# A hybrid attention layer: the third unit's queries and gate values as seven half-size products, the slot cut in two

## The chip, the cores and the metric

The kernel runs on one core of a Trainium2 chip. A core has a matrix engine (TensorE, PE in the profile, with PEld for its weight loads), a vector engine (VectorE, DVE), a scalar engine (ScalarE, ACT), GpSimd (POOL) and SyncE (SP), which here does nothing but issue DMAs. The metric is the device time of one execution in microseconds (us); lower is better.

## The reference, cut to what matters

One decoder layer over 2048 tokens of width 1024. The input is normalised and modulated to `h`, and one projection of `h` gives all that the two attention groups need:

```python
proj = jnp.einsum('bsd,de->bse', h, w_in[l])
gq, gk, gv, ga, gz, sq, sk, sv, sz = split_cols(proj, COL_SIZES)
o_gla = gla_chunked(gq, gk, gv, log_a)            # gated linear attention, 4 heads
o_gla = rmsnorm(o_gla, g_gla_head) * silu(gz)
o_swa = sliding_window_sink_attention(rope(sq), rope(sk), sv, sinks)   # 8 query heads
o_swa = o_swa * silu(sz)
y = jnp.einsum('bse,ed->bsd', jnp.concatenate([o_gla, o_swa], axis=-1), w_out[l])
x = x + gate * y                                   # then a last rmsnorm
```

The queries `sq` and the gated group's values `gv` (the "gate values" of the change) are 512 columns each, so side by side they are one product of 2048 x 1024 tokens by 1024 x 1024 weights.

## The kernel before, in words

**Numbers in two parts.** All is float32 in and out. A large product splits each factor into a rounded high part and the rest (`hh`, `hl` for the tokens; two parts of each weight), both of type float32r, and adds three products (`mm3`: high-high, high-rest, rest-high). One product of 128 x 128 by 128 x 512 is one MATMUL instruction.

**Units and slots.** The 2048 tokens go in four units `u` = 0 to 3 of 512. A unit's projection is cut into slots: `kv` (keys, values and the low-rank gate), `sz0`, `sz1`, `gz0`, `gz1` (the gates), `qk0`, `qk1` (the gated group's queries and keys), `sq` and `gv`. A 512-column slot done plainly takes 4 token tiles x 8 pieces of k x 3 = 96 MATMULs, so `sq` and `gv` take 192 in a unit. `ORDER` (L58) lists the slots of units 1 and 2, `ORDER_F` those of a unit in `FAST` (L59, L60). When the slots that a piece of attention needs are there, the main loop (from L1720) records it: sliding-window tiles (`swa_tile`, PE tiles `pq`, `psc`, `ppt`, `ppo`), the linear attention (`gla`, tiles `gaT`, `pz`, `pk`, `pc`, `pu`, `po`, `pms`).

**Seven products for eight.** Unit 3 alone is in `FAST`. There `sq` and `gv` are one slot `sqgv`: the 512 x 1024 tokens and the 1024 x 1024 weights are seen as 2 x 2 blocks, and Strassen's algorithm (in Winograd's form, `SEVEN`, L65) makes seven block products of 24 MATMULs each, 168 in all. It needs sums of token blocks, `s1` to `s4`, sums of weight blocks, `t1` to `t4`, and sums of the results.

- The token sums (`prepare`, L715) are made on DVE from the slot `sz0` on, in four steps i. A step adds `hh` and `hl` back into two buffers (tag `xs`, two buffers, tile `S`), forms the sums, splits one buffer into parts (`Shh`, `Shl`) and stores the other in DRAM (`sd`), from where `second` loads it later for `s1` and `s4`. The next step's buffers are free when that store has landed. The parts live in the five pairs of `h` buffers that the next unit's tokens, or the output weights, take afterwards.
- The weight sums (`late_cols(k)`, L672, k from 0 to 3, called 4 to 7 in `LATE_AT`) are made once: per k four loads of `wct`, four subtractions on POOL, four splits (ACT `wtxt`, DVE `wtyt`) and eight stores to `wt` in DRAM.
- The results are added as they leave PSUM (`done`, L785), by DVE, 14 adds of 128 x 512; the plain slots are taken out by DVE's rotary products (`sq`) and by ACT copies (`gv`).

**Weights.** Unit 0 splits the weights and stores both parts in DRAM (`wc`). Later units load each tile again, 1 MB as two DMAs of 512 KB, into five buffers (`WB`, L61; `ahead`, L909): the load of a tile waits until PE is done with the tile five before. A plain 512-column slot loads 4 MB; `sqgv` loads 14 tiles, 14 MB. The output weights are made alike by `late_gate` and `late_rows(k)` (k 0 to 3: four loads of `wor`, 14 stores to `woc`) and loaded by `last_rows` near the end; then come the output products (`ya`, `ys`, `yl`).

**What sets the order.** Nothing runs as it is written. Each operation is recorded (class `Order`), with the engine, a planned length, what it reads and writes, and a priority: its place in the program plus a "lift" (negative is earlier). `issue` (L229) then lays all operations out by a list schedule and writes a fixed order for each engine. SP works through one queue in that order: a DMA whose data or buffer isn't ready holds all behind it. All instructions carry the lines of the helper (L454 for MATMUL, L397 for the rest), so the tiles' names tell what is what: `w_b` are weight blocks loaded from `wc`, `w_t` the sums loaded from `wt`, `pf` the PSUM tiles of the seven products, `pn` and `pt` those of plain slots.

Of the kernel before, what the change touches and what calls it, by code (L numbers as in the profile page):

```python
# [53 lines left out]
NORM_AT0 = 'sq'  # L54
NORM_AT = 'sq'
ORDER0 = ['sz1/0', 'gz1/0', 'kv', 'sz1/1', 'gv', 'sq', 'qk1', 'gz1/1']
ORDER = ['sz0', 'kv', 'sz1', 'sq', 'qk0', 'gv', 'gz0', 'qk1', 'gz1']
FAST = (3,)  # L58
ORDER_F = {2: ['sz0','kv','sz1','sqgv','qk0','gz0','qk1','gz1'], 3: ['sz0','kv','sqgv','sz1','qk0','gz0','qk1','gz1']}  # L59
STATS_AT = 0  # L60
AGAIN_LIFT = 800  # L61
PREP_LIFT = 400
PREP_AT = 'sz0'
SEVEN = (("a11", "b11"), ("a12", "b21"), ("s2", "t2"), ("s3", "t3"), ("a22", "t4"), ("s1", "t1"), ("s4", "b22"))
LATE_AT = {(1,'sz0'):'gate',(1,'sz1'):0,(1,'sq'):4,(1,'gv'):5,(1,'qk1'):6,(2,'sz0'):7,(2,'sz1'):1,(2,'gv'):2,(2,'gz0'):3}  # L65
WO = ("b11", "b21", "t1", "b22", "t2", "t3", "t4")
# [3 lines left out]
LIFT = 600  # L70
# [332 lines left out]
def layer_kernel(ctx, tc, small, x, xT, w_ada, w_gate, b_gate, w_in, w_dec, w_out, g_fin, out):  # L403
# [289 lines left out]

    def slot_f(u):
# [17 lines left out]
        stream.extend([lambda n=n, j=j: load(n, j) for n in range(7) for j in range(2)])  # L712
        return lambda i, n, k: tiles[n, k // 2][:, k % 2, i]
# [461 lines left out]
    gv = {}  # L1175
# [538 lines left out]
    for i, (u, slot) in enumerate(todo):  # L1714
# [112 lines left out]
```

## Time and profile before

| what | value |
|---|---|
| median of 3 runs | 822.41 us (822.40 to 823.12) |
| profiled execution, its own time | 822.16 us |
| its span, first to last instruction | 820.4 us |
| granted TensorE clock | 0.998 |
| moved by DMA | 221.79 MB, 270 GB/s mean |
| unit 2 (its first `sz0` product to unit 3's) | 328.9 to 492.9 us |
| unit 3 (to its last `gz1` product) | 492.9 to 647.6 us |
| output products after that | 647.6 us to the end |

Busy time of an engine is the union of its instructions' times; MATMULs overlap one another (about 0.39 us each, a new one every 0.23 us), so PE's busy time is not a sum of lengths. "Idle before" gives the time in which the engine had nothing running ahead of an instruction, and what released it. SPq rows are DMAs as SP issues them; a long one was held at the head of the queue.

### The profile page before, as it was taken

Reading aid. Unit: us, or ns where it says so; the run is one execution under the profiler, and the core shown is the slowest. Engines: PE = TensorE matmul, PEld = TensorE weight load, DVE = VectorE, ACT = ScalarE, POOL = GpSimd, SP = SyncE. Lnnn points to the kernel's source line nnn. Section 1 sums busy time; section 2 is a strip of 40 time slices with the busy share of each in tenths; the row PEclk is TensorE's granted clock in tenths of the full one; section 3 lists DMA queues with packets and bytes.
Section 4 is the critical chain, followed back from the end, with each engine's and each line's share of the span. In section 5 each row is a group of like instructions: output and inputs, shape, how many; then the busy total and the mean of one; then the engine's idle time right before and its main releaser. Section 6 shows DMA issues by size and latency. Waiting matters only on the chain.

```text
span 820.4 us, 13492 instructions
## 1 busy us (share of the span) xinstructions
PE 803.6 (98%) x4262; PEld 669.0 (82%) x4262; DVE 626.8 (76%) x1234; ACT 528.0 (64%) x1315; POOL 377.7 (46%) x458
## 2 busy tenths in 40 slices
PE   8899999999999999999999999999999999999996
PEld 7788788888888878878887888788888888888885
DVE  6998467777668988675788958877686577989985
ACT  4769856899546787857488766453786636444432
POOL 3813225476435766656569542343644332223300
PEclk9999999999999999999999999999999999999999
DMA  9979998738286597998977967899999945664422
GB/s 357 372 257 379 380 388 290 265 130 325 100 291 233 195 371 251 303 336 307 348 278 269 324 225 235 286 353 402 340 350 346 309 128 178 218 201 153 165 99 78
DMA packets 101917, 221.79 MB, mean 270 GB/s; under 512 B 10531, under 2 KB 28502, under 8 KB 99158
## 3 DMA queue, kind: packets, MB, share of 16 engines
q1 hardware_dynamic: 101558, 220.67, 75.8%
q8 instruction: 34, 0.56, 0.3%
q14 instruction: 37, 0.30, 0.1%
q10 hardware_dynamic: 288, 0.26, 0.1%
HBM read 156.80 MB, written 64.09 MB: 269 GB/s over the span
## 4 chain that ended last, share of the span: by engine, by line
PE 76%; DMA 7%; DVE 4%; ACT 4%; issue 2%; POOL 1%; SPq 1%; DVEq 0%; POOLq 0%; ACTq 0%
PE pt L454 23%; PE pn L454 15%; PE ya L454 10%; PE ys L454 9%; PE pf L454 5%; PE ppo L454 3%; PE psc L454 3%; PE po L454 2%; PE ppt L459 2%; DMA xt<-in_xT 1%; DMA xn<-in_x 1%; PE pc L454 1%; PE pms L454 1%; DMA wr_gv<-in_w_in 1%; PE pu L454 1%
## 5 line engine op out<-in xcount | busy, mean ns | idle before, releaser
L454 PE MATMUL pt<-hh,w_gz 128*128 128x512 f32 x224 | 75.7, 397 | 0.0
L454 PE MATMUL pt<-hh,w_qk 128*128 128x512 f32 x224 | 74.5, 398 | 0.0
L454 PE MATMUL pt<-hh,w_sz 128*128 128x512 f32 x224 | 73.6, 397 | 0.3 <-ACT kvr L397 0.3
L397 ACT ACTIVATE ge<-ge 128x512 f32<-128x512 f32 x96 | 60.5, 630 | 9.8 <-DVE ge L397 8.9
L397 ACT ACTIVATE s<-s,nm 128x129 f32<-128x129 f32 x128 | 51.1, 400 | 18.4 <-DVE nm L397 17.8
L454 PE MATMUL pn<-w_gv,hh 128*128 128x512 f32 x192 | 62.0, 397 | 0.2 <-ACT kvr L397 0.2
L454 PE MATMUL pn<-w_sq,hh 128*128 128x512 f32 x192 | 61.7, 395 | 0.0
L397 POOL TENSOR_TENSOR xt<-xt,rstd 128x512 f32<-128x512 f32 x27 | 40.6, 1505 | 28.7 <-DMA xt<-in_xT 24.9
L454 PE MATMUL ys<-woht,m 128*128 128x512 f32 x168 | 53.6, 392 | 0.0
L397 POOL TENSOR_TENSOR o<-o,zs 128x128 f32<-128x128 f32 x64 | 33.5, 542 | 39.8 <-DVE o L397 29.8
L454 PE MATMUL pn<-w_kv,hh 128*128 128x272 f32 x256 | 50.1, 290 | 0.2 <-ACT zs L397 0.2
L454 PEld LDWEIGHTS pt<-hh,w_sz 128*128 128x128 f32 x224 | 41.7, 188 | 9.2 <-ACT kvr L397 0.5
L454 PE MATMUL ya<-wohb,m 128*128 128x512 f32 x152 | 49.0, 390 | 0.0
L454 PEld LDWEIGHTS pt<-hh,w_gz 128*128 128x128 f32 x224 | 41.7, 188 | 8.5 <-issue 0.2
L454 PEld LDWEIGHTS pt<-hh,w_qk 128*128 128x128 f32 x224 | 41.7, 188 | 8.3
L397 POOL TENSOR_TENSOR s<-s,den 128x512 f32<-128x512 f32 x32 | 37.7, 1181 | 16.1 <-DVE den L397 15.3
L454 PE MATMUL pt<-hl,w_gz 128*128 128x512 f32 x112 | 44.5, 397 | 0.0
L454 PE MATMUL pt<-hl,w_sz 128*128 128x512 f32 x112 | 44.4, 396 | 0.0
L454 PE MATMUL pt<-hl,w_qk 128*128 128x512 f32 x112 | 44.3, 396 | 0.0
L397 POOL TENSOR_TENSOR qr<-qr,rope 128x256 f32<-128x256 f32 x32 | 26.4, 846 | 35.4 <-DVE rope L397 25.7
L454 PEld LDWEIGHTS pn<-w_sq,hh 128*128 128x128 f32 x192 | 35.8, 188 | 8.1 <-issue 0.3
L454 PEld LDWEIGHTS psc<-kst,qs 128*128 128x128 f32 x256 | 37.7, 188 | 5.5 <-DVE s L397 1.0
(324 smaller groups left out, 2475.1 us busy)
## 6 DMA issues: line engine op xcount, KB each, us to landing
w_sz<-wc SPq DMA_DIRECT2D x24, 512.0 KB, 6.2
w_qk<-wc SPq DMA_DIRECT2D x24, 512.0 KB, 5.1
w_gz<-wc SPq DMA_DIRECT2D x24, 512.0 KB, 5.1
w_sq<-wc SPq DMA_DIRECT2D x16, 512.0 KB, 7.0
w_gv<-wc SPq DMA_DIRECT2D x16, 512.0 KB, 9.1
w_t<-wt SPq DMA_DIRECT2D x16, 512.0 KB, 7.4
mr<-mixd SPq DMA_DIRECT2D x32, 256.0 KB, 3.6
y<-in_x SPq DMA_DIRECT2D x32, 256.0 KB, 3.3
```

Source lines behind the costliest of these rows:

```text
L397: return order.add(eng, lambda: real(*args, **kw), dur, ins, outs, lock=lock, nbytes=nbytes)
L454: return od.add("PE", lambda: T.matmul(o, l, r, start=start, stop=stop), dur, [l, r] + ([] if start else [o]), [bank if start and bank is ...
L459: return od.add("PE", lambda: T.transpose(o, i, ident), 0.109, [i, ident], [o], mode="few" if o.shape[0] <= 32 else None)
```

## The change

Four things change together.

1. Unit 2 joins `FAST`: its `sq` and `gv` become seven products too. `prepare(2)` is called at its `sz0`.
2. The slot of the seven products is cut: `sqgv` makes the first five (a11 b11, a12 b21, s2 t2, s3 t3, a22 t4: all queries are there after them), a new slot `gvb` makes the last two (s1 t1, s4 b22). Unit 2 has `qk0` between them, unit 3 `qk0` and `qk1`. In both units `sz1` now stands ahead of `sqgv`; before, unit 3 had it behind. What waited for `gv`, and the next unit's `norm`, comes after `gvb`.
3. `LATE_AT` is rewritten: the weight sums (4 to 7) are recorded in unit 1 (second of the four, slots `sz0` and `kv`) ahead of the gate (`qk0`), the output weights (0 to 3) in unit 2 from `gz0` to unit 3's `sz0`. Before, the gate came first, and sums and output weights alternated from unit 1's `sz1` to unit 2's `gz0`.
4. `AGAIN_LIFT`, the priority of `second`, goes from 800 to 600.

```diff
-FAST = (3,)
-ORDER_F = {..., 3: ['sz0','kv','sqgv','sz1','qk0','gz0','qk1','gz1']}
+FAST = (2,3)
+ORDER_F = {2: ['sz0', 'kv', 'sz1', 'sqgv', 'qk0', 'gvb', 'gz0', 'qk1', 'gz1'],
+           3: ['sz0', 'kv', 'sz1', 'sqgv', 'qk0', 'qk1', 'gvb', 'gz0', 'gz1']}
-AGAIN_LIFT = 800
+AGAIN_LIFT = 600
-LATE_AT = {(1,'sz0'):'gate',(1,'sz1'):0,(1,'sq'):4,(1,'gv'):5,...}
+LATE_AT = {(1, 'sz0'): (4, 5), (1, 'kv'): (6, 7), (1, 'qk0'): 'gate', ...}
...
+    SPLIT = 5
+    def part_of(u, slot):
+        at = SPLIT if "gvb" in ORDER_F[u] else len(SEVEN)
+        return range(at) if slot == "sqgv" else range(at, len(SEVEN))
...
-        for n, (a, _) in enumerate(SEVEN):
+        def product(n, a, w):
...
+        def run(slot, w):
+            for n in part_of(u, slot):
+                product(n, SEVEN[n][0], w)
...
-        if u < NU - 1 and name == ("sqgv" if u in FAST else NORM_AT if u else NORM_AT0):
+        if u < NU - 1 and (last_f if u in FAST else name == (NORM_AT if u else NORM_AT0)):
```

How the order moves, first in SP's queue at the start of unit 3's `kv`. Before, the stores of the token sums (`sd`) stand directly ahead of the first product's second weight tile (`w_b_1`):

```order
L397 DMA w_kv_3_1403<-wc 128x544 x2
L397 DMA woc<-woyb_1296 128x512
L397 DMA w_b_0_1407<-wc 128x1024 x2
L397 DMA sd_104<-S_1395 128x512
L397 DMA sd_104<-S_1397 128x512
L397 DMA w_b_1_1432<-wc 128x1024 x2
L397 DMA w_b_0_1433<-wc 128x1024 x2
L397 DMA w_b_1_1434<-wc 128x1024 x2
L397 DMA sd_104<-S_1399 128x512
```

Now, at the same place:

```order
L397 DMA w_kv_3_1420<-wc 128x544 x2
L397 DMA mixd<-o 128x256
L397 DMA sd_105<-S_1412 128x512
L397 DMA woc<-woyt_1361 128x512
L397 DMA w_sz_0_1424<-wc 128x1024 x2
L397 DMA woc<-woyb_1363 128x512
L397 DMA sd_105<-S_1414 128x512
L397 DMA wor_1366<-in_w_out 128x512
L397 DMA woc<-woxt_1364 128x512
L397 DMA w_sz_1_1467<-wc 128x1024 x2
L397 DMA w_b_0_1468<-wc 128x1024 x2
```

The second store now stands ahead of `sz1`'s second tile, and the products' tiles come after it.

The same place in unit 2, SP's queue from the last `kv` tile on. Before, plain weights, token loads for the next unit's statistics (`xn`) and the weight sums under way (`wct` in, `wt` out):

```order
L397 DMA w_kv_3_980<-wc 128x544 x2
L397 DMA wt<-wtyt_829 128x512
L397 DMA wct_890<-in_w_in 128x512
L397 DMA xn_1198<-in_x 128x512
L397 DMA wt<-wtxt_830 128x512
L397 DMA mixd<-qk_834 128x4x128
L397 DMA w_sz_0_984<-wc 128x1024 x2
```

Now:

```order
L397 DMA w_kv_3_993<-wc 128x544 x2
L397 DMA woc<-woxb_1292 128x512
L397 DMA sd_104<-S_985 128x512
L397 DMA w_sz_0_997<-wc 128x1024 x2
L397 DMA woc<-woyb_1293 128x512
L397 DMA sd_104<-S_987 128x512
L397 DMA w_sz_1_1022<-wc 128x1024 x2
L397 DMA w_b_0_1023<-wc 128x1024 x2
L397 DMA w_b_1_1024<-wc 128x1024
L397 DMA sd_104<-S_989 128x512
L397 DMA w_b_1_1024<-wc 128x1024
L397 DMA w_b_0_1025<-wc 128x1024 x2
```

The weight sums are gone from here (they stand in unit 1 now), the statistics' loads come some twelve rows later, and three stores of token sums stand among the weight tiles.

PE's rows in unit 2, where the first token tile of `gv` began, before (one tile `pn` runs through all eight `h` pieces; a piece of sliding-window work, `ppo`, stands between):

```order
L454 MATMUL pn_1231<-w_gv_1_1070,hh_2_811 128x512 x2
L454 MATMUL pn_1231<-w_gv_1_1070,hl_2_812 128x512
L454 MATMUL pn_1231<-w_gv_1_1070,hh_3_814 128x512
L454 MATMUL ppo<-ph,vs 128x512
L454 MATMUL pn_1231<-w_gv_1_1070,hh_3_814 128x512
L454 MATMUL pn_1231<-w_gv_1_1070,hl_3_815 128x512
```

Now, where the second product ends and the third, with token sums, begins (a piece of linear attention, `pms`, stands between):

```order
L454 MATMUL pf_1064<-w_b_0_1025,hh_3_819 128x512 x2
L454 MATMUL pf_1064<-w_b_0_1025,hl_3_820 128x512
L454 MATMUL pf_1064<-w_b_1_1034,hh_5_962 128x512
L454 MATMUL pms<-osq_948,ones_r 128x512
L454 MATMUL pf_1064<-w_b_1_1034,hh_5_962 128x512
L454 MATMUL pf_1064<-w_b_1_1034,hl_5_963 128x512
L454 MATMUL pf_1064<-w_b_1_1034,hh_7_968 128x512 x2
L454 MATMUL pf_1064<-w_b_1_1034,hl_7_969 128x512
L454 MATMUL pf_1069<-w_t_0_1038,Shh_974 128x512 x2
```

A `pf` tile takes four pieces of k, 12 MATMULs, where a `pn` tile takes eight, 24. Unit 2 has 14 `pf` tiles in place of 8 `pn` tiles, 168 MATMULs in place of 192.

More of the change, by code (lines that the diff above doesn't have):

```diff
@@ L57 @@
 ORDER = ['sz0', 'kv', 'sz1', 'sq', 'qk0', 'gv', 'gz0', 'qk1', 'gz1']
-FAST = (3,)
-ORDER_F = {2: ['sz0','kv','sz1','sqgv','qk0','gz0','qk1','gz1'], 3: ['sz0','kv','sqgv','sz1','qk0','gz0','qk1','gz1']}
+FAST = (2,3)
+ORDER_F = {2: ['sz0', 'kv', 'sz1', 'sqgv', 'qk0', 'gvb', 'gz0', 'qk1', 'gz1'], 3: ['sz0', 'kv', 'sz1', 'sqgv', 'qk0', 'qk1', 'gvb', 'gz0', 'gz1']}
 STATS_AT = 0
-AGAIN_LIFT = 800
+AGAIN_LIFT = 600
 PREP_LIFT = 400
@@ L64 @@
 SEVEN = (("a11", "b11"), ("a12", "b21"), ("s2", "t2"), ("s3", "t3"), ("a22", "t4"), ("s1", "t1"), ("s4", "b22"))
-LATE_AT = {(1,'sz0'):'gate',(1,'sz1'):0,(1,'sq'):4,(1,'gv'):5,(1,'qk1'):6,(2,'sz0'):7,(2,'sz1'):1,(2,'gv'):2,(2,'gz0'):3}
+LATE_AT = {(1, 'sz0'): (4, 5), (1, 'kv'): (6, 7), (1, 'qk0'): 'gate', (2, 'gz0'): 0, (2, 'qk1'): (1, 2), (3, 'sz0'): 3}
 WO = ("b11", "b21", "t1", "b22", "t2", "t3", "t4")
@@ L692, in late_cols, with slot_f @@
         part("t4", b[1, 0], b[1, 0], b[1, 1])
-    def slot_f(u):
+    SPLIT = 5
+    def part_of(u, slot):
+        at = SPLIT if "gvb" in ORDER_F[u] else len(SEVEN)
+        return range(at) if slot == "sqgv" else range(at, len(SEVEN))
+    def slot_f(u, slot):
         tiles = {}
@@ L710, in load @@
                 SY.dma_start(f(t[:, k]), f(src))
-        stream.extend([lambda n=n, j=j: load(n, j) for n in range(7) for j in range(2)])
+        stream.extend([lambda n=n, j=j: load(n, j) for n in part_of(u, slot) for j in range(2)])
         return lambda i, n, k: tiles[n, k // 2][:, k % 2, i]
@@ L751, in prepare, with proj_f @@
         return combos, second
-    def proj_f(u, w, combos, qr_of):
+    def proj_f(u, combos, qr_of):
         def left(op, k, p):
@@ L826, in proj_f @@
                 od.lift = 0
+        def run(slot, w):
+            for n in part_of(u, slot):
+                product(n, SEVEN[n][0], w)
+        return run
     def rope_in_place(q, t):
@@ L1652, in layer_kernel @@
     todo = [(0, n) for n in ORDER0] + [(u, n) for u in range(1, NU) for n in (ORDER_F[u] if u in FAST else ORDER)]
-    ws = [slot_f(u) if n == "sqgv" else slot_w(u, n, LIFT if i > 1 else 0) for i, (u, n) in enumerate(todo)]
-    ready_s = {}
+    ws = [slot_f(u, n) if n in ("sqgv", "gvb") else slot_w(u, n, LIFT if i > 1 else 0) for i, (u, n) in enumerate(todo)]
+    ready_s, run_f = {}, {}
     warm(WARM0, None)
@@ L1724, in layer_kernel @@
             qrs[u] = {}
-            proj_f(u, w, ready_s[u], qrs[u])
+            run_f[u] = proj_f(u, ready_s[u], qrs[u])
+            run_f[u](name, w)
+        elif name == "gvb":
+            run_f[u](name, w)
         elif name == "sq":
@@ L1734, in layer_kernel @@
         seen.add((u, slot))
-        seen |= {(u, n) for n in ("sq", "gv") if name == "sqgv"}
+        if name == "sqgv":
+            seen.add((u, "sq"))
+        last_f = u in FAST and name == ("gvb" if "gvb" in ORDER_F[u] else "sqgv")
+        if last_f:
+            seen.add((u, "gv"))
         if half:
@@ L1746, in layer_kernel @@
                               ("Z", 0, ("qk0", "gz0", "gv")), ("Z", 1, ("qk1", "gz1", "gv"))):
-            if (name in need or name == "sqgv") and all((u, n) in seen for n in need):
+            if (name in need or "sq" in need and name == "sqgv" or "gv" in need and last_f) and all((u, n) in seen for n in need):
                 if what == "S":
```

## Prediction

> **What bounds the kernel now.** I read the page first, its busy times and the chain that ended last.
>
> ```profile
> PE 803.6 (98%) x4262; PEld 669.0 (82%) x4262; DVE 626.8 (76%) x1234; ACT 528.0 (64%) x1315; POOL 377.7 (46%) x458
> PE 76%; DMA 7%; DVE 4%; ACT 4%; issue 2%; POOL 1%; SPq 1%; DVEq 0%; POOLq 0%; ACTq 0%
> ```
>
> PE is busy 98% of the span and holds 76% of the chain. A busy PE need not be a fast one, since the MATMULs overlap, so I looked at the pace next: two pieces of the chain in which one slot's products stand alone, the first plain, the second of the seven products.
>
> ```profile
> 98.00 12.75 PE pn L454 x56
> ...
> 560.73 5.49 PE pf L454 x24
> ```
>
> 12.75/56 = 0.228 us and 5.49/24 = 0.229 us for a MATMUL of 512 columns, in both kinds of slot. Then the waits of PE, the longest four of its list, to see what is left besides work:
>
> ```profile
> PE po L454 <- ACT hh L397: 2.3, 2, 2.1
> PE pw L454 <- POOL ones_r L397: 2.1, 1, 2.1
> PE pf L454 <- DMA w_b<-wc: 1.7, 1, 1.7
> PE pk L459 <- DVE qk L397: 1.2, 1, 1.2
> ```
>
> The first two belong to the start, which the change leaves. Of the rest only the third, in unit 3's seven products, is over 1.2 us. So the time is the number of MATMULs by their pace, and the question is whether PE is still fed. For that I read the busy times by stage: unit 2, unit 3, the densest 10 us of DMA that I found, and two stretches inside unit 3 that matter below.
>
> ```profile
> 330.00:492.90 162.90, 161.17 (x898) 134.17 (x897) 122.00 (x224) 115.84 (x287) 100.09 (x114) 1.00 0.84 298
> 492.90:647.80 154.90, 153.13 (x850) 128.04 (x849) 115.34 (x241) 95.39 (x242) 67.60 (x84) 1.00 0.93 326
> 400.00:410.00 10.00, 10.00 (x60) 8.82 (x59) 6.99 (x16) 7.52 (x24) 5.15 (x6) 1.00 1.03 406
> 505.60:516.00 10.40, 10.35 (x85) 9.98 (x86) 8.45 (x24) 4.82 (x13) 1.28 (x4) 1.00 0.46 132
> 516.00:560.00 44.00, 42.29 (x234) 34.65 (x231) 35.88 (x73) 19.55 (x38) 19.59 (x24) 1.00 0.98 353
> ```
>
> After the length come PE, PEld, DVE, ACT and POOL, the clock, the DMA share and GB/s. DVE runs at 75% in both units (122.00/162.90, 115.34/154.90), and DMA is the next limit: 353 GB/s at a share of 0.98 while unit 3's seven products load their weights.
>
> **Part by part.** *Fewer products.* Unit 2's `sq` and `gv` go from 192 to 168 MATMULs (14 `pf` tiles of 12). 24 x 0.229 = 5.5 us leave the engine that sets the end. The other work of PE is the same in number.
>
> [...]
>
> *Unit 3's wait.* SP's queue and PE at the start of unit 3's products, with the landing of the load that PE waited for:
>
> ```profile
> 504.56 0.41 PE L454 MATMUL pn<-w_kv,hh 128*128 128x272 f32 x2
> ...
> 518.52 0.62 PE L454 MATMUL pf<-w_b,hh 128*128 128x512 f32 x2
> ...
> 522.24 0.73 PE L454 MATMUL pf<-w_b,hh 128*128 128x512 f32 x2 [1.71 <-DMA w_b<-wc]
> ```
>
> ```profile
> 504.75 0.80 SPq L397 DMA_DIRECT2D w_b<-wc  x2
> 505.64 10.43 SPq L397 DMA_DIRECT2D sd<-S  x2
> 516.16 3.34 SPq L397 DMA_DIRECT2D w_b<-wc  x6
> 522.89 0.32 SPq L397 DMA_DIRECT2D sd<-S  x1
> ```
>
> ```profile
> 516.16 6.03 DMA w_b<-wc
> ```
>
> The second store of token sums stood 10.43 us at the head of the queue; the tile behind it was issued at 516.16, landed 6.03 us later at 522.19, and PE had wanted it 1.71 us before 522.24, at 520.5. Now `sz1` stands between `kv` and the products, and behind the second store comes `sz1`'s second tile. PE wants that 24 MATMULs after `kv`, at 518.5 + 5.5 = 524.0: 1.8 us to spare. The product's second tile now stands behind the third store: 522.9 + 0.3 + 6.0 = 529.2, wanted at 518.5 + 11.0 (`sz1`) + 1.4 (six MATMULs) = 530.9: 1.7 us to spare. So the wait of 1.7 us goes. It stays, in another place, if the stores come 1 us later each.
>
> *The same chain, new in unit 2.* `prepare` and its stores stand there as in unit 3, with one half of the second tile ahead of the third store, so the spare time is no smaller. What differs is the bytes. From the first store to the last tile of the fifth product the queue holds 17.3 MB by the sizes in its order: tiles 12.6, stores 1.0, statistics' loads (`xn`) 2.1, the rest 1.6. With K the start of `kv`, that last tile is wanted at K + 14.0 (`kv`, 518.52 - 504.56) + 11.0 (`sz1`, 48 x 0.229) + 23.4 (102 MATMULs) + 6.0 (other PE work in the slot, an estimate from the rows below and from 14 small ones) = K + 54.4.
>
> ```profile
> 477.52 1.02 PE pu L454 x16
> ...
> 528.00 1.09 PE pc L454 x16
> ...
> 536.60 1.99 PE po L454 x24
> ```
>
> If the first 10.4 us go at 132 GB/s, as unit 3's did while the store held the queue (1.4 MB), the remaining 15.9 MB take 39.2 us at 406 GB/s or 45.0 us at 353. The tile lands at K + 1 + 10.4 + 39.2 = K + 50.6, in time, or at K + 56.4, 2.0 us late. I take the middle of no wait and 2.0: +1.0 us. For unit 3 the queue holds 17.0 MB (no `xn`, more output weights): none or 1.2 us, I take +0.6.
>
> *DVE and ACT in unit 2.* The token sums and the adds cost what unit 3's did:
>
> ```profile
> L397 DVE TENSOR_TENSOR S<-hh,hl 128x512 f32<-128x512 f32 x8 | 6.6, 822 | 4.2 <-DMA sd<-S 4.1
> L397 DVE TENSOR_TENSOR S<-S,S 128x256 f32<-128x256 f32 x12 | 6.1, 510 | 0.1
> L397 DVE TENSOR_TENSOR Shl<-S,Shh 128x512 fp32r<-128x512 f32 x8 | 6.1, 772 | 1.3 <-PE pms L454 0.7 <-ACT Shh L397 0.6
> L397 DVE TENSOR_TENSOR S<-S 128x256 f32<-128x256 f32 x4 | 1.7, 415 | 0.0
> L397 DVE TENSOR_TENSOR v<-pf,v 128x512 f32<-128x512 f32 x4 | 2.7, 686 | 2.4 <-PE pf L454 2.4
> L397 DVE TENSOR_TENSOR wtyt<-wct,wtxt 128x512 fp32r<-128x512 f32 x16 | 14.2, 890 | 2.9 <-ACT wtxt L397 1.4 <-issue 1.1 <-DMA w_kv<-wc 0.3
> L397 DVE TENSOR_TENSOR wtyt<-wct,wtxt x16: 678/691/1777, 327.7 to 427.4; 128x512 fp32r<-128x512 f32 x16
> ```
>
> 6.6 + 6.1 + 6.1 + 1.7 = 20.5 us, and 14 adds x 0.686 = 9.6. But the 14.2 us of splitting weight sums, all but the first of which ran in unit 2 (327.7 to 427.4), move to unit 1. Net 122.0 + 30.1 - 14.2 = 138 us of DVE in some 157: 88%. A `pf` tile lives 12 MATMULs, 2.75 us, and its adds take 0.69 or 1.4; PE's list has no wait for them in unit 3. I cost this at nothing; PE's own work covers it, and if the cover goes, it shows as the late stores below.
>
> *Moves.* Unit 2's queue holds 2.2 MB less than before (45.9 for 48.1, weight sums out, the larger tiles in), all from unit 3's first tile on holds 4.3 MB more (70.1 for 65.8, late output weights). Sums made early in unit 1 load POOL, busy 46% of the span. The 1.2 us wait of `pk` stood in unit 2 and may go or come back elsewhere: 0, from -1.2 to +1.2.
>
> Sum: 822.16 (the profiled execution; the runs' median, 822.41, is as good as the same) - 5.5 - 1.7 + 1.0 + 0.6 = **816.6 us**.
>
> **The rivals.**
>
> *DMA becomes the bound; the gain is given back.* The queue is already at 0.93 to 0.98 where this change adds. If it goes at 340 GB/s, between unit 3's mean of 326 and the 353, unit 2's last tile lands at K + 11.4 + 46.8, 3.8 us late, unit 3's (15.6 MB after the slow start) at K + 57.3, 2.9 us late; the 4.3 MB more in the last stage take 12.2 us at 353 where 7% of 154.9, 10.8 us, are free: 1.4 more. 822.16 - 5.5 - 1.7 + 8.1 = 823.1: no difference that counts. For it: the shares. Against: before, 16.8 MB went through the same place with one wait, and that came of the queue's order.
>
> [...]
>
> *The stores of token sums come later, and weights wait behind them; slower.* The steps were 8.6 us on average ((522.89 - 505.64)/2). In unit 2 the second half of the product's second tile lands at K + 1.1 + two steps + 6.0 and is wanted at about K + 27.1, so this decides from 10.0 us a step. At 14 us, were DVE 5 us a step busier with other work: `sz1`'s second tile 1.9 us late, that half tile 6.1 more, the tile behind the fourth store 1.1: 9.1 us. In unit 2 alone that is 822.16 - 5.5 - 1.7 + 9.1 = 824.1, in both units 833.2. For it: DVE at 88%, and thin spare times. Against: the weight sums are out of the way, and unit 3's steps were made beside much the same work.
>
> **How the numbers follow.** A difference of 0.2%, 1.6 us, is about what a measurement here can tell from none: faster is below 820.8, slower above 824.1. My forecast, with waits up to 5.8 us in all, has 0.74; the DMA bound, within 0.2%, 0.14; late stores, slower, 0.12. The range: at the low end no new wait and `pk`'s gone, 822.16 - 5.5 - 1.7 - 1.2 = 813.8; at the high end it reaches to the DMA bound short of its full price, 822.8; late stores and a little of the DMA case stay outside.
>
> **What would show it.** Right: PE has 4238 instructions; `pf` takes 0.229 us in unit 2 too; the list of PE's waits no longer has 1.7 us for `w_b` in unit 3, and DMA waits of `pf` and of unit 2's and 3's `sz` sum to under 3 us. The DMA rival: waits of `pf` on `w_t`, or of `ya` on `woc`, with a share near 1 at the time. The late stores: SP rows of `sd` of over 10 us each, and PE waiting for `sz` or `w_b` right behind them. Wrong altogether: PE's idle time elsewhere, as in unit 1, grown by more than 3 us.

## The result, and the profile after

The changed kernel takes 828.71 us (median of 5 runs, 826.57 to 831.03) where the kernel before takes 822.41 us beside it (5 runs, 822.08 to 823.29). The ratio is 1.0072, with an interval of 1.0053 to 1.0092: slower by 6.3 us, where 5.8 us less was forecast. The profiled execution took 829.09 us, its span 827.0. (Of one experiment below, `e5_unit3_order`, the profiled execution was a disturbed one, with a span of 990.7 us, so only the times of its other 11 are used.)

Busy times and the chain that ended last, from the page of after:

```profile
PE 802.8 (97%) x4238; PEld 667.3 (81%) x4238; DVE 648.9 (78%) x1280; ACT 534.3 (65%) x1321; POOL 373.6 (45%) x458
PE 72%; DVE 12%; ACT 6%; DMA 6%; issue 3%; POOL 1%; SPq 0%; ACTq 0%; DVEq 0%; POOLq 0%
```

The 24 MATMULs are gone (4262 before), but the chain now goes through VectorE for 12% of the span, where it was 4%. PE's list of waits in the trace of after (us in total, times, longest) says where:

```profile
PE pk L459 <- DVE qk L397: 2.7, 2, 2.2
PE pq L459 <- DVE qs L397: 2.4, 2, 2.1
...
PE ppo L454 <- ACT ph L397: 1.4, 2, 0.8
PE pt L454 <- DVE hl L397: 1.2, 1, 1.2
PE pn L454 <- DMA w_kv<-wc: 1.1, 1, 1.1
PE psc L454 <- DVE s L397: 1.1, 1, 1.1
```

The wait for `w_b` is gone, and none for a Strassen weight came in its place. The new waits are for results of VectorE and ScalarE. By stage, unit 1 of before first, then units 1, 2 and 3 of after (length, busy times of PE, PEld, DVE, ACT, POOL, granted clock, DMA share, GB/s); units 2 and 3 of before stand in the prediction:

```profile
158.80:328.90 170.10, 169.76 (x935) 142.44 (x934) 132.05 (x270) 127.64 (x352) 102.25 (x132) 1.00 0.67 236
```

```profile
157.10:336.20 179.10, 172.47 (x928) 143.33 (x927) 136.39 (x269) 133.38 (x365) 113.44 (x142) 0.99 0.75 258
336.20:487.50 151.30, 150.38 (x823) 125.70 (x822) 123.44 (x253) 107.95 (x268) 71.64 (x89) 1.00 0.86 305
487.50:654.00 166.50, 162.50 (x926) 135.31 (x925) 132.47 (x263) 105.47 (x263) 75.98 (x94) 0.99 0.90 314
```

Unit 1, whose products the change leaves alone, is 9.0 us longer with seven PE instructions fewer. Units 2 and 3 hold different shares of the work, so their lengths can't be compared alone. For them I worked out an **excess** from the starts of all MATMULs: the gap from each start to the next, less the median gap that the same kind of MATMUL has in before, summed by stage (a stage begins with the first `sz0` MATMUL of its unit). The medians themselves, summed, are the MATMULs' own time.

| stage | before: own time, excess | after: own time, excess |
|---|---|---|
| up to unit 1 | 150.3, 6.4 | 149.1, 5.9 |
| unit 1 | 164.5, 5.7 | 164.4, 14.7 |
| unit 2 | 156.6, 7.4 | 146.1, 5.1 |
| unit 3 | 148.1, 6.6 | 154.9, 11.7 |
| output products | 163.6, 1.6 | 163.4, 1.7 |

The own time fell by 5.2 us in all, what 24 MATMULs cost. The excess rose by 11.4 us: 9.0 in unit 1, 5.1 in unit 3, less 2.3 in unit 2 and 0.4 elsewhere.

**Unit 1.** The loss stands within 20 us, where the sliding-window attention of unit 0 ends beside unit 1's first slot `sz0` (tile `pt`). PE's timeline there, before and then after (`pq` turns a query tile, `ppt` a score tile):

```profile
167.41 0.38 PE L459 MATMUL pq<-ident,qr 128*128 128x128 f32 x2
...
169.25 0.60 PE L459 MATMUL ppt<-ident,s 128*128 128x128 f32 x4
...
173.83 0.38 PE L459 MATMUL pq<-ident,qr 128*128 128x128 f32 x2
```

```profile
172.85 0.51 PE L454 MATMUL pt<-hl,w_sz 128*128 128x512 f32 x1 [1.25 <-DVE hl L397]
...
174.94 0.38 PE L459 MATMUL pq<-ident,qr 128*128 128x128 f32 x2
175.39 0.73 PE L454 MATMUL pt<-hh,w_sz 128*128 128x512 f32 x2
178.23 0.66 PE L459 MATMUL pq<-ident,qr 128*128 128x128 f32 x2 [2.11 <-DVE qs L397]
178.69 1.06 PE L459 MATMUL ppt<-ident,s 128*128 128x128 f32 x4
```

Before, 17 `pt` MATMULs and some pieces of attention lie between the two query tiles, 6.4 us of work in which ScalarE and VectorE make the next one ready. After, two `pt` MATMULs lie between the same two tiles, and PE stands for 2.11 us.

**Unit 3.** The chain of after ahead of its longest wait (start, length):

```profile
521.29 0.47 DVE S L397
521.75 0.03 DVE vdf L397
521.78 5.88 DMA sd<-S
527.67 0.02 issue
527.69 0.69 DVE S L397
...
531.63 0.61 DVE qk L397
532.25 0.04 issue
532.29 0.84 PE pk L459 x4
```

The next step's addition `S` reuses the buffer that a store of token sums is reading. It can't start until the store has landed, 5.88 us after its issue, and all that stands behind it in VectorE's queue waits too, `qk` among it, which PE needs. VectorE itself had other work for most of that time; its own timeline has it idle for 1.25 us:

```profile
527.69 0.69 DVE L397 TENSOR_TENSOR S<-hh,hl 128x512 f32<-128x512 f32 x1 [1.25 <-DMA sd<-S]
```

### The profile page after: what moved, and what is told of

Its sections match the earlier page's. It is cut to its first block, busy times and chain, and to the rows that moved or that the text cites. A ratio compares the mean times of both kernels' runs of the same rounds, so it can differ in the third digit from the quotient of the medians.

```text
span 827.0 us, 13500 instructions
## 1 busy us (share of the span) xinstructions
PE 802.8 (97%) x4238; PEld 667.3 (81%) x4238; DVE 648.9 (78%) x1280; ACT 534.3 (65%) x1321; POOL 373.6 (45%) x458
## 4 chain that ended last, share of the span: by engine, by line
PE 72%; DVE 12%; ACT 6%; DMA 6%; issue 3%; POOL 1%; SPq 0%; ACTq 0%; DVEq 0%; POOLq 0%
PE pt L454 19%; PE pn L454 10%; PE ys L454 9%; PE ya L454 9%; PE pf L454 8%; PE po L454 6%; PE ppo L454 3%; PE psc L454 2%; PE ppt L459 1%; DMA sd<-S 1%; DMA xn<-in_x 1%; PE pc L454 1%; PE pu L454 1%; DVE S L397 1%; ACT ge L397 1%
## 5 line engine op out<-in xcount | busy, mean ns | idle before, releaser
L454 PE MATMUL pt<-hh,w_gz 128*128 128x512 f32 x224 | 72.7, 394 | 0.0
L397 ACT ACTIVATE ge<-ge 128x512 f32<-128x512 f32 x96 | 60.6, 631 | 16.9 <-DVE ge L397 15.7
L397 ACT ACTIVATE s<-s,nm 128x129 f32<-128x129 f32 x128 | 51.0, 399 | 11.3 <-DVE nm L397 10.9
L397 POOL TENSOR_TENSOR xt<-xt,rstd 128x512 f32<-128x512 f32 x27 | 37.9, 1407 | 23.1 <-DMA xt<-in_xT 17.1
L397 POOL TENSOR_TENSOR s<-s,den 128x512 f32<-128x512 f32 x32 | 34.7, 1086 | 29.0 <-DVE den L397 24.0
L454 PE MATMUL psc<-kst,qs 128*128 128x256 f32 (+1 forms) x256 | 43.0, 286 | 1.2 <-DVE s L397 1.1
L397 ACT ACTIVATE junk<-y 128x512 f32<-128x512 f32 x31 | 19.5, 631 | 37.3 <-DVE y L397 29.8
L454 PEld LDWEIGHTS pn<-w_kv,hh 128*128 128x128 f32 x256 | 41.1, 189 | 2.4 <-DMA w_kv<-wc 1.3
L454 PE MATMUL pn<-w_sq,hh 128*128 128x512 f32 x128 | 41.8, 398 | 0.0
```

The source lines that it names most:

```text
L397: return order.add(eng, lambda: real(*args, **kw), dur, ins, outs, lock=lock, nbytes=nbytes)
L454: return od.add("PE", lambda: T.matmul(o, l, r, start=start, stop=stop), dur, [l, r] + ([] if start else [o]), [bank if start and bank is ...
```

## The experiments

Two theories came out of this. **A**: the weight sums, which `LATE_AT` now puts at the border of units 0 and 1, crowd the vector engines there. **B**: in unit 3 the addition holds VectorE's queue until the store lands. The rival to both: any new order costs some waits, and these are only where they fell. In the tables "before" is the median of the kernel before on the same chip.

### One part of the change alone

`e1_late_only` is the kernel before with the new weight schedule; `e5_unit3_order` and `e13_unit2_plain` are the changed kernel with unit 2 done plainly, the former with the old weight schedule too.

```diff
 # e1_late_only, against before
-LATE_AT = {(1,'sz0'):'gate',(1,'sz1'):0,(1,'sq'):4, ...
+LATE_AT = {(1,'sz0'):(4,5),(1,'kv'):(6,7),(1,'qk0'):'gate', ...
 # e5_unit3_order and e13_unit2_plain, against after
-FAST = (2,3)
+FAST = (3,)
 # e5_unit3_order besides
-LATE_AT = {(1,'sz0'):(4,5),(1,'kv'):(6,7),(1,'qk0'):'gate', ...
+LATE_AT = {(1,'sz0'):'gate',(1,'sz1'):0,(1,'sq'):4, ...
```

> The kernel before with the change's LATE_AT alone: weight sums recorded in unit 1's sz0 and kv, seven products in unit 3 only. Theory A (the early weight sums crowd DVE, ACT and POOL where unit 0's sliding window and the next unit's norm end, and PE waits there): PE waits of 0.8 to 2.3 us around 165 to 190 us again, some 7 to 9 us of loss, 828 to 831 us. Rival (the place of the sums is harmless, the loss in unit 1 comes with the new order of the seven products): 822.4 within 1.6 us, no PE wait over 0.5 us between 150 and 190.

> The changed kernel with seven products in unit 3 only and LATE_AT as before: what is left of the change is unit 3's order, its slot in two parts and the priority of the second sums. As forecast: the 1.7 us wait for w_b goes, 820.7 us. Theory B: pk waits for DVE in unit 3 as in the changed kernel and the clock falls, 2 to 5 us of loss against that, 822.5 to 826 us. Theory A alone: 820 to 822.5, no wait between 150 and 190.

> The changed kernel with unit 2 by the plain products again (24 MATMULs more, no token sums of unit 2), the weights' early schedule and unit 3's new order kept. It parts the change in three with two runs that stand: early weights alone 834.9 beside 822.9, unit 3's order alone 821.5 beside 822.9. If the shares add, this is 833 to 834, and Strassen's products in unit 2 by themselves are worth 5 to 6 us, the 5.5 us of the prediction. Rival (the three disturb each other and no share holds by itself): 828 or less, or 837 or more.

| run | time (runs) | before | ratio, interval | unit 1's excess |
|---|---|---|---|---|
| e1_late_only | 834.93 (4) | 822.91 | 1.0145, 1.0126 to 1.0164 | 12.9 |
| e5_unit3_order | 821.35 (11) | 822.91 | 0.9981, 0.9970 to 0.9991 | no trace |
| e13_unit2_plain | 830.52 (6) | 823.98 | 1.0083, 1.0064 to 1.0102 | 14.1 |

The schedule of the weights alone costs 1.45%, 12 us, more than the 7 to 9 that theory A had, with the same waits at the border (0.8, 1.0 and 2.2 us by the starts, between 167 and 178 us); unit 3's new order alone costs nothing. So unit 1's loss comes with the new schedule of the weights, in which gate and output weights moved as well; that it is the sums, `e6_sums_held` shows below. But the shares do not add. From 834.93 to 830.52 only unit 3's order differs, 0.6% where it was worth 0.2% by itself, and from 1.0083 to after's 1.0072 Strassen's products in unit 2 are worth 0.9 us, with intervals of some 1.6 us each, not 5.5. The 830.52 us lie between what the third expectation named for shares that add (833 to 834) and for shares that don't (828 or less).

### The sums and the gate in other places

Five kernels move them, by the table alone or, in `e6_sums_held`, with a dependency that the scheduler sees on the last MATMUL of a slot:

```diff
 # e2_sums_later
+LATE_AT = {(1,'sz1'):4,(1,'sq'):5,(1,'qk0'):6,(1,'gv'):7,(1,'gz1'):'gate', ...
 # e6_sums_held
+LATE_AT = {(1,'kv'):4,(1,'sz1'):5,(1,'sq'):(6,7),(1,'qk0'):'gate', ...
-            SY.dma_start(b[r, c], src[:, 2 * k + r])
+            SY.dma_start(b[r, c], src[:, 2 * k + r]).deps.add(held[0])
 # e9_gate_first, e10_gate_first_spread
+LATE_AT = {(1,'sz0'):'gate',(1,'kv'):(4,5),(1,'sz1'):(6,7), ...
+LATE_AT = {(1,'sz0'):'gate',(1,'sz1'):4,(1,'sq'):5,(1,'qk0'):6,(1,'gv'):7, ...
 # e15_sums_unit0
+LATE_AT = {(0,'kv'):(4,5),(0,'gv'):(6,7),(1,'sz0'):'gate',(1,'sz1'):0, ...
```

> The changed kernel with the weight sums recorded one by one behind unit 1's sz1, sq, qk0 and gv instead of two each behind sz0 and kv, the gate behind gz1. Theory A: the waits between 160 and 190 us go, 828.7 less 7 to 9 is 819.5 to 822 us; unit 3's wait of pk stays. Rival (order noise: any new laying out loses as much somewhere): 826 to 831.

> The changed kernel, with the weight sums of Strassen's products held back for certain: the loads of a group's weights wait for the last MATMUL of a named slot of unit 1 (kv, sz1, sq, sq), so no sum can be made before about 199 us, when the border of units 0 and 1 is past; the gate and the output weights are recorded where they were. The first experiment on this moved only the order of recording, and the sums stayed where they were. Theory A (sums at the border of units 0 and 1 crowd VectorE, ScalarE and GpSimd, and PE waits there): the waits of 0.6 to 2.1 us between 165 and 180 us and the half clock after them go, PE's excess in unit 1 falls from 14.7 to about 6, and the time to 819 to 821. Rival (unit 1 loses wherever the sums are made, since the engines there have no room for them): the waits come again later in unit 1 and the time stays at 826 to 829. Theory B (the loss in unit 3 is VectorE's queue held by the store of the token sums): the 2.2 us wait of pk at about 525 stays, so not under 818.

> The changed kernel with the gate of the output weights back at its place of before (recorded in unit 1 behind sz0) and the weight sums recorded behind it, so that they come after the gate on every queue (from about 270 us) and before unit 2's Strassen slot; the output weights stay where the change put them. Holding the sums alone took the waits at the border of units 0 and 1 away (unit 1's excess 14.7 to 6.9) but put the gate late, and unit 2's excess rose from 5.1 to 16.6. Theory A' (what costs is that sums or gate fall on a border where the attention's last steps need the same engines): with the gate at 228 to 272 us and the sums at 272 to about 360 us both borders have room, unit 1's excess is 6 to 7 and unit 2's 5 to 8, and the time 818 to 821. Rival (no room anywhere: the S additions of unit 2's token sums, some 20 us of VectorE, are what overfills it): unit 2's excess is 12 or more and the time 825 to 829.

> The same with the four sums recorded further apart (behind sz1, sq, qk0 and gv), so that the last of them come between unit 2's first products. Theory A': about the same, 818 to 822, if the w_t loads still land in time; a wait of PE for w_t between 390 and 430 us, 1 to 4 us, if not, and 822 to 826. Rival (no room): 825 to 829, with the waits elsewhere.

> The changed kernel with the weight sums recorded in unit 0 (behind kv and gv, so that they start some 30 to 40 us earlier and most of them come before the border), the gate and the first part of the output weights at their places of before, and the other parts late as in the change. Theory A (the loss is the place, the border, where ScalarE and VectorE have no room): unit 1's excess falls from 14.7 to 6 to 9 and the time to 820 to 824. Rival (the sums' loads and stores meet unit 0's weights, whose DMA share is 0.88 to 1.0 there, and PE waits for weights instead; or unit 2's additions meet the output weights): 827 or more.

| run | time (runs) | before | ratio, interval | excess of units 1, 2 | sums (`wtyt`) run |
|---|---|---|---|---|---|
| e2_sums_later | 853.96 (4) | 822.91 | 1.0379, 1.0360 to 1.0398 | 15.6, 20.7 | 142.7 to 290.7 |
| e6_sums_held | 828.19 (6) | 822.52 | 1.0066, 1.0051 to 1.0081 | 6.9, 16.6 | 215.3 to 320.2 |
| e9_gate_first | 845.63 (5) | 823.14 | 1.0270, 1.0241 to 1.0299 | 4.9, 29.3 | 281.4 to 364.1 |
| e10_gate_first_spread | 840.12 (5) | 823.14 | 1.0209, 1.0181 to 1.0237 | 5.8, 29.9 | 279.7 to 411.4 |
| e15_sums_unit0 | 872.36 (5) | 822.72 | 1.0607, 1.0587 to 1.0627 | 5.8, 9.0 (48.1 ahead of unit 1) | 97.6 to 194.2 |

`e2_sums_later` didn't move the first sums (they run from 142.7 us on, in after from 143.1: the list schedule filled them in at the border all the same), so it decides nothing on A; its new layout costs 25 us, most of it in unit 2 and later. `e6_sums_held` did move them. Here are 10 us of the border in before, in after and in that run:

```profile
168.00:178.00 10.00, 10.00 (x64) 8.87 (x63) 7.48 (x15) 9.63 (x23) 5.72 (x10) 1.00 0.67 216
```

```profile
168.00:178.00 10.00, 6.09 (x24) 3.56 (x22) 7.23 (x12) 9.03 (x23) 10.00 (x12) 0.98 0.46 149
```

```profile
168.00:178.00 10.00, 10.00 (x62) 8.91 (x61) 6.38 (x14) 9.78 (x29) 5.23 (x9) 1.00 0.50 150
```

With the sums away PE is busy for all 10.00 us again (6.09 in after), and GpSimd for 5.23 (10.00). ScalarE is nearly full in all three, 9.03 to 9.78: this is where the kernel before had no room, though ScalarE's share of the span is 64%. But the time didn't fall. The gate, behind the sums in the same ring of buffers, ended at 361 us instead of 343, beside unit 2's token sums, and PE waited there instead, as its list of waits between 345 and 385 us has it:

```profile
PE pms L454 <- ACT osq L397: 2.6, 2, 1.3
PE pg L454 <- ACT ga L397: 1.7, 1, 1.7
PE pf L454 <- ACT zs L397: 1.4, 1, 1.4
```

The same went for the rest. With the gate first (`e9_gate_first`) PE waited 10.0 us at one place in unit 2 for ScalarE's `kvr`, and in unit 0 (`e15_sums_unit0`) 14.4 us for ScalarE's `w_sq`, the split of weights that had come late. First e9, then e15:

```profile
PE pt L454 <- ACT kvr L397: 10.0, 1, 10.0
```

```profile
PE pn L454 <- ACT w_sq L397: 14.4, 1, 14.4
```

Theory A's price for a better place, 818 to 824 us, failed four times. That after loses at the border, and only with the sums planned there, is shown; that there is a free place elsewhere is not.

### The store and the additions

`e3_st_buffer` gives the stored half another ring of buffers, `e7_sd_slow` tells the scheduler that the store takes 4 us longer, `e8_held_slow` adds the held sums of e6 to that, and `e14_no_store` takes the stores away from the additions: as many are made near the start, of other data (`e16_unit0_no_store` does so with the sums in unit 0).

```diff
 # e3_st_buffer
-                x1, x2 = [stp.tile([P, NB], F32, name=f"S{i}{c}{u}", tag="xs", bufs=2) for c in range(2)]
+                x1 = stp.tile([P, NB], F32, name=f"S{i}0{u}", tag="xs", bufs=2)
+                x2 = stp.tile([P, NB], F32, name=f"S{i}1{u}", tag="st")
 # e7_sd_slow, e8_held_slow
+                SY.dma_start(sd[u][:, i], x2).slow = 4.0
-        t = d.end + HOP[o.eng] + ...
+        t = d.end + d.slow + HOP[o.eng] + ...
 # e14_no_store, e16_unit0_no_store
-                SY.dma_start(sd[u][:, i], x2)
+    for u in FAST:                         # once, near the start
+        for i in range(KT // 2):
+            SY.dma_start(sd[u][:, i], cos.rearrange("p a b -> p (a b)"))
```

> The changed kernel with the stored buffer of the token sums taken from the ring st (three buffers) instead of xs (two), so that a step of sums does not wait for the store before it to land. Theory B (in unit 3 the next step's first add stands at the head of DVE's queue until the store lands, the linear attention's key product stands behind it, PE waits 2.2 us for it and its clock is halved for 3.4 us after): pk's wait in unit 3 under 0.5 us, no lowered clock there, 4 us less, 824 to 825.5 us. Rival (DVE is simply full there): 828.7 within 1.6.

> The changed kernel, with the store of the token sums taken by the scheduler as 4 us longer, so that the next step's S additions, which wait for it on the chip, are put behind other work of VectorE instead of ahead of it. Nothing else is changed; the sums of the weights stay early. Theory B: the 2.2 us wait of pk in unit 3 (532 us) and the half clock behind it go, unit 3's excess falls from 11.7 to about 8, and the time to 824 to 826. Theory A alone (the border only): 828 to 829. Rival: the token sums come late for the Strassen products, PE waits for S or its splits instead, and the time is 829 to 832.

> Both edits together: the weight sums held until unit 1's kv, sz1 and sq are done, and the stores of the token sums taken as 4 us longer. Theories A and B, if their shares add: 828.7 less 9 less 3 to 4, 815 to 817, which is what the prediction's sum gave. If only A holds: 819 to 821. If neither, and any new order costs some waits: 825 or more.

> The changed kernel without the stores of the token sums from their buffers in units 2 and 3: their place in memory is filled once, near the start, with other data, so the second halves of the sums that are loaded again are not the right ones; all additions, splits and products remain. No addition can then wait for a store to land. Theory B (VectorE's queue is held by the next addition until the store lands): the 2.2 us wait of pk in unit 3 and the 3.4 us at half clock behind it go, unit 3's excess falls from 11.7 to about 8, and the time to 824 to 826. If the additions themselves hold pk up and not the store: 828 to 829.

> The last two together: sums in unit 0, gate at its old place, and no stores of the token sums (so the second halves of these are not the right ones). Theories A and B, if their shares add: 816 to 820. If only the place counts: as the run with the sums in unit 0 alone.

| run | time (runs) | before | ratio, interval | excess of units 1, 2, 3 |
|---|---|---|---|---|
| e3_st_buffer | 846.80 (5) | 822.91 | 1.0293, 1.0274 to 1.0313 | 15.7, 4.2, 26.8 |
| e7_sd_slow | 836.58 (4) | 822.52 | 1.0173, 1.0158 to 1.0189 | 13.7, 16.7, 5.6 |
| e8_held_slow | 842.39 (4) | 822.52 | 1.0235, 1.0217 to 1.0253 | 7.1, 23.0, 10.6 |
| e14_no_store | 846.97 (5) | 822.72 | 1.0310, 1.0289 to 1.0331 | 21.6, 7.6, 17.5 |
| e16_unit0_no_store | 876.94 (5) | 822.72 | 1.0661, 1.0637 to 1.0684 | 5.2, 14.4, 6.1 |

All five miss. `e7_sd_slow` did take `pk`'s wait out of unit 3 (excess 5.6) and lost more in unit 2. The plainest is `e14_no_store`: no addition could wait for a store any more, and it is 18 us slower than after, with a wait of 7.7 us in unit 3 for the very `qk` that it should have freed:

```profile
PE pk L459 <- DVE qk L397: 7.7, 1, 7.7
```

With other things ready at other planned times, the scheduler had laid out all engines anew. `e12_no_sum_work` shows the same for theory A. It leaves out the arithmetic of the weight sums:

```diff
-            G.tensor_tensor(to, x, y, ALU.subtract)
-            A.copy(parts[0], to)
-            V.tensor_tensor(parts[1], to, f(parts[0]), ALU.subtract)
             for j in range(2):
-                SY.dma_start(f(wt[:, int(op[1]) - 1, k // 2, k % 2, j]), f(parts[j]))
+                SY.dma_start(f(wt[:, int(op[1]) - 1, k // 2, k % 2, j]), (x, y)[j])
```

> The changed kernel without the arithmetic of the weight sums: the loaded weight blocks are stored as they are where the halves of the sums stood, so GpSimd's 16 subtractions, ScalarE's 16 roundings and VectorE's 16 remainders of them are left out (the products of the T combinations then take plain weight blocks); their loads and stores, and Strassen's products with them, are as many as before. Theory A (the vector engines' work of the sums, done early): the waits at the border of units 0 and 1 go and the time is 816 to 821. Rival (the loss is that of the later gate and output weights, or of the token sums of unit 2, or of the loads): still 825 or more.

It took 839.48 us (5 runs, before 823.98, ratio 1.0190, 1.0169 to 1.0212), the rival's side and beyond it: unit 1's excess is 9.8, but unit 2's 15.7 and unit 3's 12.7, with 11.3 us of waits for `qk`. None of these edits can tell what the thing taken away had cost.

### The order kept

So the last three keep every instruction of the changed kernel at its place on PE, VectorE, ScalarE and GpSimd: the scheduler sees the operation as it was, and only what is sent to the chip differs. In their traces the instructions of these four engines stand in the order of after, without exception.

```diff
 # e17_no_hold: the store reads a buffer that nothing reuses
-                SY.dma_start(sd[u][:, i], x2)
+                o = SY.dma_start(sd[u][:, i], x2)
+                o.fn = lambda i=i: nc.sync.dma_start(sd[u][:, i], cos.rearrange("p a b -> p (a b)"))
 # e18_thin_sums: a = slice(0, 2), so for ScalarE and VectorE too; the stores send `to`
-            G.tensor_tensor(to, x, y, ALU.subtract)
+            o = G.tensor_tensor(to, x, y, ALU.subtract)
+            o.fn = lambda: nc.gpsimd.tensor_tensor(to[:, a], x[:, a], y[:, a], ALU.subtract)
 # e19_both: both
```

> The changed kernel, instruction by instruction in its own order on every engine; only the stores of the token sums read another buffer of the same size (so the second halves that are loaded again are not the right ones). No addition of VectorE then waits for a store to land; traffic and all other work are the same. Theory B: the 2.2 us wait of pk in unit 3 and the 3.4 us at half clock behind it go, and the time is 824 to 826. If the additions themselves hold pk up and not the store: 828 to 829.

> The changed kernel in its own order on every engine; only the 48 operations of the weight sums (GpSimd's subtraction, ScalarE's rounding, VectorE's remainder) work on 2 columns instead of 512, and the stores send the unfinished blocks, so Strassen's T products take wrong weights. Every instruction, load and store stays, at its place. Theory A (the time of this work at the border of units 0 and 1): the waits of 0.6 to 2.1 us between 165 and 180 us and the half clock go, unit 1's excess falls from 14.7 to 6 to 8, and the time to 819 to 822. Rival (not the time of the sums but the order that the scheduler made around them, or their DMAs, costs it): 826 or more.

> Both edits at once, the order still that of the changed kernel. If A and B are the whole loss: 814 to 818, which holds the forecast of 816.6. If A alone counts: 819 to 822. If neither: 826 or more.

| run | time (runs) | before | ratio, interval | excess of units 1, 2, 3 |
|---|---|---|---|---|
| e17_no_hold | 823.81 (12) | 822.69 | 1.0010, 0.9992 to 1.0027 | 15.3, 4.1, 6.5 |
| e18_thin_sums | 826.25 (12) | 822.69 | 1.0041, 1.0023 to 1.0059 | 15.7, 6.8, 10.7 |
| e19_both | 823.16 (12) | 822.69 | 1.0003, 0.9986 to 1.0020 | 13.0, 4.8, 8.5 |

**Theory B holds.** The ratio falls by 0.62 points from after's 1.0072, 5.1 us (the two intervals are some 1.5 us each way), a little over the 3 to 5 expected. The chain of e17 at the place of the long wait:

```profile
525.67 0.18 DVE vdf L397
525.86 0.60 DVE S L397
...
529.71 0.61 DVE qk L397
530.32 0.04 issue
530.37 0.66 PE pk L459 x4
```

`S` follows straight on `vdf`. In its list of waits `pk` has 0.8 us where it had 2.7, the half clock there is gone, and unit 3 takes 161.30 us instead of 166.50:

```profile
486.90:648.20 161.30, 160.49 (x925) 134.38 (x924) 132.19 (x263) 105.38 (x262) 76.69 (x94) 1.00 0.92 326
```

Of the 5.2 us by which unit 3's excess falls, 2.8 stand in the 20 us around this wait, about what the shorter wait (1.3 us) and the full clock (1.7) make. Two later waits of after, at 619 us (`psc` for VectorE's `s`, 1.1 us) and at 632 us (`ppo` for ScalarE's `ph`, 0.8 us), are gone as well; how they hang on the hold isn't shown. The edit does one thing more: the store no longer waits for `S`, so SyncE's queue is freed too. PE waited for no weight in unit 3 of after, which speaks against a gain from that, but no run separates the two.

**Theory A, as the time of the sums' work, falls for the larger part.** With 2 columns for 512 the sums' 48 operations are short (those at the border take 0.15 to 0.36 us each, for medians of 1.30 on GpSimd, 0.62 on ScalarE and 0.69 on VectorE in after), and the border's waits are still there. PE's timeline of e18:

```profile
174.22 0.38 PE L459 MATMUL pq<-ident,qr 128*128 128x128 f32 x2
174.37 0.73 PE L454 MATMUL pt<-hh,w_sz 128*128 128x512 f32 x2
176.94 0.41 PE L459 MATMUL pq<-ident,qr 128*128 128x128 f32 x2 [1.84 <-DVE qs L397]
```

1.84 us for 2.11. GpSimd is no longer full there, 6.47 of 10 us, and PE is busy for 6.86 where it had 6.09:

```profile
168.00:178.00 10.00, 6.86 (x32) 4.58 (x31) 6.99 (x13) 8.51 (x24) 6.47 (x11) 1.00 0.55 163
```

Between 160 and 190 us the excess is 9.3 us in after, 9.0 in e17, 7.2 in e18 and 6.2 in e19, and under 1 in before and in e6: the work takes 2 to 3 of the 9 us, and the rest stays. (The 15.7 of e18 for all of unit 1 holds another 3.9 us between 300 and 310, 0.6 in after, where the clock of that execution stood at half for 3.4 us, with a mean of 0.98 over unit 1 for 0.99 in after; it was the longest of e18's twelve, 831.02 us.) In time the work of the sums is worth 0.31 points, 2.5 us, by e18 and 0.07, 0.6 us, once B is gone (e19 against e17), with intervals of some 2 us on each. The 823.16 us of e19 fit none of the three cases that its expectation named: B's part is gone, A's hardly. What stays is that the scheduler, with the sums planned there, left two `pt` MATMULs between two query tiles where there had been 17. That is the rival of e18's expectation. It has a second half, the sums' loads and stores; e18 kept them, and no run separates them from the order. The chain of e18 passes through no DMA from 159.7 to 179.0 us, which speaks for the order.

### A wait made on purpose

The granted clock of after reads 0.5 for 3.4 us behind two of its waits (rows of windows; the first began at 177.65 us, before its wait ended):

```profile
178.20:181.10 2.90, 2.87 (x10) 2.61 (x11) 1.32 (x2) 1.33 (x5) 0.72 (x2) 0.51 0.79 200
...
532.60:536.00 3.40, 3.40 (x12) 2.64 (x10) 2.47 (x4) 1.70 (x3) 0.00 (x0) 0.50 1.02 339
```

So two waits were put into the kernel before, with the rest of the program as it was (the scheduler moved a small part of it: some 250 of PE's 4262 MATMULs stand elsewhere in the order):

```diff
...
+    def emit():
+        T.matmul(p[:, 0:16], ones, ident[:, 0:16], start=True, stop=True)
+        nc.vector.tensor_copy(pf, p[:, 0:16])
+        for k in range(n):                     # n = 5 in unit 1, 14 in unit 2
+            nc.gpsimd.memset(pf, 0.0)
+        return T.matmul(p[:, 16:32], ones, pf, start=True, stop=True)
```

> The kernel before, with two waits put into PE's queue on purpose and nothing else: ahead of gz0 of units 1 and 2 a small MATMUL goes to PSUM, VectorE copies it, GpSimd writes the copy 5 times (unit 1) or 14 times (unit 2), and the next MATMUL reads it, so that PE stands still for some 1.5 us and some 3 us. Nothing of the result changes. Theory of the clock: the long wait is followed by about 3.4 us at half clock, which costs 1.7 us beyond the wait, and the short one by none; the time is that of before plus both waits plus 1.7. Rival (the half clock seen behind the waits of the changed kernel has another cause): before plus the two waits, clock 1.0 behind both.

It took 836.40 us (5 runs) beside 823.14, ratio 1.0168 (1.0134 to 1.0202). The two waits in PE's timeline, and the clock behind them:

```profile
346.57 0.61 PE L1723 MATMUL pw<-pos_f,ones_r 128*128 128x16 f32 x2 [3.72 <-POOL pos_f L1722]
...
505.97 0.39 PE L1723 MATMUL pw<-pos_f,ones_r 128*128 128x16 f32 x2 [3.93 <-POOL pos_f L1722]
```

```profile
345.90:352.70 6.80, 6.08 (x25) 5.87 (x26) 1.63 (x3) 2.77 (x6) 0.44 (x5) 0.50 0.91 297
...
506.30:509.70 3.40, 3.34 (x9) 2.60 (x9) 1.83 (x4) 2.45 (x5) 0.00 (x0) 0.50 0.00 0
```

Both waits came out near 4 us, since VectorE and GpSimd had other work queued (at the first GpSimd was busy for 2.96 of 3.90 us, its five writes 0.11 each; at the second VectorE for 1.86 of 4.00), so the short one was not tried. 3.72 + 3.93 us of waiting and half of 6.8 + 3.4 us at half clock make 12.8 us; the runs differ by 13.3. By the starts, 7.2 and 6.3 us of excess stand at the two places, so the moved part counts for little. In these traces a wait of PE of 2 to 4 us costs itself and, where the clock falls, 1.7 or 3.4 us more, half of the 3.4 or 6.8 us at half clock.

## Why the prediction was wrong

- **24 MATMULs less, 5.5 us: right.** PE has 4238 instructions, the own time of the MATMULs fell by 5.2 us, and in unit 2 a piece of the chain with nine `pf` MATMULs takes 2.07 us, 0.230 each:

```profile
394.28 2.07 PE pf L454 x9
```

- **Unit 3's wait for `w_b`, 1.7 us: right.** It is in no list of after.
- **Late weights, +1.0 and +0.6 us: too dear.** PE waited for no `w_b`, `w_t` or `w_sz`; its one wait for a weight was 1.1 us for `w_kv` in unit 1, behind the border. The DMA rival (823.1) fell with it: shares of 0.86 and 0.90 in units 2 and 3, and no wait.
- **VectorE in unit 2, 138 of 157 us:** it was 123.44 of 151.30, as harmless there as it was costed.
- **"Sums made early in unit 1 load POOL, busy 46% of the span": the first failed step.** It costed a move at nothing by an engine's share of the whole span. Where the sums landed, GpSimd went from 5.72 to 10.00 of 10 us, ScalarE was at 9.63 before, and PE went from 10.00 to 6.09. Unit 1's excess rose by 9.0 us. e6 shows that it comes with the sums planned there; e18 that the time of their work is 2 to 3 of the 9, and the rest the order laid around them, or their DMAs.
- **`pk`'s wait, "0, from -1.2 to +1.2": the second.** It became 2.2 us in unit 3 with 3.4 us of half clock behind it; at a fixed order, taking the hold away is worth 5.1 us, 2.8 of them at that wait. The prediction's own row of `S<-hh,hl` had 4.1 us of VectorE idle behind these stores, and no term priced what stands behind such a hold; in after it is 2.2 us in two waits, so the loss isn't the hold's length but what stands behind it.
- **The late stores, the second rival: half came.** It had looked at the same stores and seen only SP's queue. That queue was held for them, longer in all than before: 20.4 us for 10.0 (rows below, before and then after; us, times, longest). The steps were 9.8, 11.1 and 10.8 us in unit 3, for the 8.6 that it used. (A row of SP shows a hold only where it merges several DMAs, as the one of 10.43 us does for a hold of 9.7; ahead of a single DMA the hold is a gap between rows.) But PE waited for no weight behind them. The queue whose hold PE felt was VectorE's.

```profile
SPq L397 <- DVE S L397: 10.0, 2, 9.7
```

```profile
SPq L397 <- DVE S L397: 20.4, 7, 6.1
```

- 816.6, less the 1.6 us for late weights that didn't come, plus 9.0 in unit 1, plus 6.8 in unit 3 (its excess rose by 5.1 although the 1.7 for `w_b` went), less 2.3 in unit 2 and 0.4 elsewhere, plus 0.3 that the MATMULs fell short, is 828.4; the profiled execution took 829.09. The text's own sign for "wrong altogether", PE's idle time grown by more than 3 us in unit 1, is what came.

Neither kernel is the fastest seen. Unit 3's new order without the rest (e5) is 0.2% below before, 0.1 to 0.3%, and that is all of the change that is worth keeping as it stands; with the hold of the stores gone the whole change is level with before (e17), not ahead, and before has such holds too and was not run without them.

## What to carry to other kernels

Cost a moved operation where it lands, and not by its engine's share of the span. Its own time may be the smaller part there (2 to 3 of 9 us here): look at what the new order leaves between two steps of a chain, 17 independent MATMULs before and two after. In a queue that goes in order, an operation that reuses a buffer under a store holds all behind it (here the store took 5.88 us to land, and PE waited 2.2 us for `qk` behind the addition), so ask what stands behind it and who waits for that. And where a scheduler lays out the program, an experiment that changes its input changes everything: with the addition's wait for the store taken away, the time rose by 18 us with a new order (e14) and fell by 5 with the old one (e17).

## What the runs showed of the hardware

The half clock came behind PE waits of 2.1 us (178.2 us in after), and stood at 0.50 for 3.4 us there, for 6.8 and 3.4 us in e11 and for 10.2 us in e6, from 371.8 us on. In e11 it began before the wait ended (at 345.9, the wait ending at 346.6). A wait of 2.1 us that ended at 22.7 us was followed by it in after, from 24.05 us on, for 3.4 us; the same wait in before, ending at 23.1 us, was not (1.00 from there to 30 us). So the length of the wait alone didn't decide it here.

VectorE's remainder of a weight sum took 1.52 us beside GpSimd's work, here in the timeline of after; its median in before is 0.69:

```profile
174.74 1.49 POOL L397 TENSOR_TENSOR s<-s,den 128x512 f32<-128x512 f32 x1
...
175.25 1.52 DVE L397 TENSOR_TENSOR wtyt<-wct,wtxt 128x512 fp32r<-128x512 f32 x1
```

GpSimd had 0.98 us left when the remainder began, and the remainder took that and 0.55 us more. The 32 remainders of before and after go the same way: the 14 that began with GpSimd idle took 0.68 or 0.69 us, and the 18 that began beside GpSimd took what GpSimd had left and about 0.55 us, and 0.69 us at the least (1.77 us with 1.23 left at 272.1 us of after). No view shows why.
